# Token-major products in 512 output columns instead of 256, and dilated queries and keys written in residue order

## The chip, the cores and the metric

The kernel runs on one core of one Trainium2 chip. The metric is device time in microseconds (us) for one execution. TensorE is called PE here (its weight loads PEld), VectorE DVE, ScalarE ACT, GpSimd POOL, and SyncE, which issues most DMAs, SP.

## The reference

A network of three layers works on 512 tokens of width 1024, all in float32. Layer A mixes gated linear attention and dilated attention, then has an MLP and a gated embedding. Layer B mixes an mLSTM and stick-breaking attention; layer C has trailing-window pools and a projection. What the change touches:

```
hatt = (rmsnorm(x) @ w_in)[..., attention columns]     # [512, 3 groups, q/k/v, 4 heads, 128]
for g, (win, dil) in enumerate(((128, 1), (512, 4), (2048, 16))):
    # query t attends to t, t-dil, ..., within the window; keys gathered by stride dil
    out_g, lse_g = dilated_attention(q_g, k_g, v_g, bias_g, dil, win // dil)
o_att = sum over g of softmax(lse)_g * out_g
v_gla  = rmsnorm(x) @ w_in[:, 1024 columns]            # gated linear attention
va, vb = rmsnorm(x1) @ w_in_ab[:, 1024 columns each]   # mLSTM, stick-breaking
out    = x2 + rmsnorm((mixed * silu(z)) @ w_out_c)     # [512, 2048] @ [2048, 1024]
```

## The kernel before

**Products.** Activations lie feature-major: a tile holds 128 features on partitions and 512 tokens. Every float32 operand of a projection is split into a high and a low part of a narrower kind (`split`, ACT writes the high part, DVE the low one), and a product is three matmuls, high*high, high*low and low*high (`mm3`, L450 on; `mm`, L156, issues each, so nearly all PE work has line L157). Each matmul has its own weight load.

**Weights** stream from memory in chunks of 128 x 1024 (512 KB), 314 of them, in the order of use. `load_chunk` (L204) issues the DMA on SP, `split_chunk` splits it. Three raw and four split chunks fit (`RAW_BUFS`, `HL_BUFS`), so a chunk is split once the chunk four before it is used up.

**Units.** Each chunk is one unit of PE work. `fm` makes a feature-major tile [128 columns, 512 tokens]: 24 matmuls with 128 weight columns as the stationary operand and 512 tokens moving, into one bank of PSUM. `tok` makes a token-major output: here the *activations* are the stationary operand, 128 tokens at a time (j = 0 to 3), and 256 weight columns move; a chunk holds four k-tiles of 256 columns and needs 48 matmuls. Its four outputs of 256 columns share two banks. With `z` set (attention groups 1 and 2), token tile j holds the tokens j, j+4, j+8, ...: the weight load then reads every fourth element of the activation tile. `by_token` (only the last output columns of layer C) goes through the last two chunks once per token tile, so that a tile's output can leave while PE works on the next.

**Token-major outputs.** The values of the attention, for two pairs of heads and three groups (`v_units(pair, g)`; six of 256 columns, 4 of them with `z`), the values of the gated linear attention (4), VA and VB of layer B (4 each, one of each in each round `a0` to `a3`), and the final output (4, with 16 k-tiles in place of 8).

**PSUM.** Eight banks: four in the pool `mm` for the units, taken in turn, and four in the pool `q` for side work. A unit's result leaves its bank by its evacuation, on ACT or DVE.

**Side work** (attention, gla, mlstm, stick, one generator per head) advances by stages: `pump` runs once per unit, a slot, and lets a stage go once its slots (`LAG`) have passed and banks are free. A planner of the framework then puts the instructions of each engine in order by its own estimate of when they are ready, so a later matmul can stand ahead of an earlier one.

**Attention.** `qk_unit` writes a head's queries and keys for each group in the order of tokens, by one DVE instruction from PSUM. For groups 1 and 2, `attention` multiplies residue class by residue class, `zs(q[g])[:, z]` with `zs(k[g])[:, z]`, plain float32: both operands are read with a stride of four elements. Two records in the trace are one such product.

**Layer B, round a.** Four units of queries and keys for the mLSTM, each evacuated by DVE (a product with `rb_`, then three multiply-adds of a convolution), then VA (2 units), VB (2 units), and two pairs of units for the stick-breaking heads.

Of the kernel before, what the change touches and what calls it, by code (L numbers as in the profile page):

```python
# [17 lines left out]
P = 128  # L18
# [24 lines left out]
# key tile j meets the queries from WIDE[j][1] on, WIDE[j][0] of them, in bank and column PLACE[j]  # L43
# [6 lines left out]
# slots of 2 KB: for the units and for two kinds of side work  # L50
# [10 lines left out]
# slots that side work lets pass before each of its stages  # L61
# [4 lines left out]
N_ONEHOT = sum(BIASW)  # L66


class Net:
# [15 lines left out]
    # ---- storage  # L85
# [25 lines left out]
    # ---- engine shorthands  # L111
    # while set, an engine takes its instructions in the order in which they are written
# [8 lines left out]
    # each x (with its bias) becomes ln(1 + exp(-|x|)), in one table set  # L121
# [65 lines left out]
    # zero where the query is not after (or not at or after) the key  # L187
# [12 lines left out]
    # ---- the weight stream  # L200
# [19 lines left out]
    # a load that takes its turn in the weight stream  # L220
# [3 lines left out]
    # ---- program building  # L224
# [3 lines left out]
    # joint: so many units of the group advance together over their k-tiles, then the others in turn;  # L228
    # halves: all of them for the first half of the tokens, then for the second
# [12 lines left out]
    # Side work is a generator per head. It yields (slots to let pass, banks of the side  # L242
    # pool that it is about to take, condition) before each of its stages on the tensor engine.
# [80 lines left out]
    # a feature-major output tile [128 columns, 512 tokens] over 8 k-tiles  # L324
# [23 lines left out]
    # at most 64 columns: their weights come twice, and the low parts take the place of the second  # L348
    # ones, so that one pass of the array serves both parts
# [27 lines left out]
    # several feature-major tiles with few k-tiles in one chunk  # L377
# [26 lines left out]
    # a token-major output of 256 columns: chunks of four k-tiles; z: tokens in residue order;  # L404
    # by_token: so many last chunks are gone through once per token tile
    def tok(self, wname, lead, col, xs, z, evac, nk=8, by_token=0):
        st = {}
        parts = nk // 4
# [6 lines left out]
        def out(j):  # L415
            if by_token:
                return st["ps"][j][:, 0:256]
            return st["ps"][j // 2][:, (j % 2) * 256:(j % 2) * 256 + 256]

        fs = {}  # L420

        def mk(part):
            def emit(h, l):
                if part == 0:
                    st["ps"] = [self.MM(), self.MM()]
                    if by_token:
                        st["ps"] += [self.Q(), self.Q()]
                for k in range(4):
                    xh, xl = xs[part * 4 + k]
                    w = slice(k * 256, (k + 1) * 256)  # L430
                    for j in range(4):
                        s = part == 0 and k == 0 and (by_token > 0 or j % 2 == 0)
                        e = part == parts - 1 and k == 3
                        fs[part, k, j] = lambda o=out(j), a=(sel(xh, j), sel(xl, j)), b=(h[:, w], l[:, w]), s=s, e=e: (
                            self.mm3(o, a, b, s, e))
                if part < parts - by_token:
                    return [[fs[part, k, j] for j in range(4)] for k in range(4)]
                if part < parts - 1:
                    return [[]]
                return [[fs[p, k, j] for p in range(parts - by_token, parts) for k in range(4)]  # L440
# [3 lines left out]
        def ev():  # L444
            for j in range(4):
                evac(j, out(j))
# [5 lines left out]
        for u in us[:parts - by_token]:  # L452
            self.group(u)
# [1192 lines left out]
```

## Time and profile before

| What | Value |
|---|---|
| median of three timed runs | 1991.83 us (1990.28 to 1995.2) |
| profiled execution, first to last instruction (span) | 1988.3 us |
| PE busy | 1968.5 us, 99% |
| PEld busy | 1700.9 us, 86% |
| DVE busy, ACT busy | 1086.8 us (55%), 870.6 us (44%) |

The page gives no time of the profiled execution beyond its span; the median of the timed runs lies 3.5 us above it. An engine's busy time is the union of its instructions. Where instructions of one kind follow each other without a gap, the time of one is found as (busy time less the duration of one) / (count less one): each instruction lasts longer than the distance to the next, because they overlap.

### The profile page before, as it was taken

What the parts mean: (1) busy time and instruction counts of PE and PEld (TensorE: products, weight loads), DVE (VectorE), ACT (ScalarE), POOL (GpSimd) and SP (SyncE); (2) the same over time, 40 slices, a digit from 0 to 9 for tenths busy, and PEclk for the clock granted to TensorE, in tenths of its full rate; (3) what the DMA queues carried; (4) which work ended last, traced back from release to release, by engine and by line L of the source; (5) the groups of instructions that cost most, each with busy time, mean ns of one, the idle gap of its engine ahead of it and who ended that gap; (6) DMA issues with size and microseconds to landing.
All of it is one profiled execution on the core that took longest, in us unless ns stands there. A gap on an engine that the chain in (4) does not pass through costs nothing.

```text
span 1988.3 us, 25237 instructions
## 1 busy us (share of the span) xinstructions
PE 1968.5 (99%) x10142; PEld 1700.9 (86%) x10142; DVE 1086.8 (55%) x1647; ACT 870.6 (44%) x1325; POOL 94.3 (5%) x125
## 2 busy tenths in 40 slices
PE   8999999999999999999999999999999999999998
PEld 7989889888888888888888988898898888888898
DVE  5042253467744643344447767676857726666733
ACT  4132234456423432243235757576656534433322
POOL 0000000000000100000103001010000011000000
PEclk9999999999999999999999999999999999999999
DMA  5231232222234233333323322222222331333331
GB/s 180 82 92 54 80 91 75 85 75 75 85 95 138 96 96 95 101 104 95 96 96 117 107 75 86 86 84 74 81 90 75 107 115 64 99 102 96 95 107 64
DMA packets 68105, 184.47 MB, mean 93 GB/s; under 512 B 17058, under 2 KB 20815, under 8 KB 67988
## 3 DMA queue, kind: packets, MB, share of 16 engines
q1 hardware_dynamic: 67412, 181.82, 29.1%
q8 instruction: 79, 1.29, 0.3%
q10 hardware_dynamic: 576, 1.05, 0.1%
q14 instruction: 38, 0.31, 0.1%
HBM read 178.55 MB, written 6.12 MB: 93 GB/s over the span
## 4 chain that ended last, share of the span: by engine, by line
PE 95%; DVE 2%; ACT 1%; DMA 1%; issue 0%; SPq 0%; POOL 0%; DVEq 0%; ACTq 0%; POOLq 0%
PE t L157 95%; DVE t L136 2%; ACT t L119 1%; DVE t L148 0%; PE t L984 0%; DMA t<-t 0%; DMA t<-wstream 0%; PE t L1552 0%; POOL t L508 0%; PE t L1056 0%; SPq L537 0%; SPq L534 0%; DVEq L1642 0%; ACT t L1531 0%; SPq L523 0%
## 5 line engine op out<-in xcount | busy, mean ns | idle before, releaser
L157 PE MATMUL t<-t,t 128*128 128x512 f32 (+1 forms) x9780 | 1928.3, 359 | 13.9 <-ACT t L119 9.2
L157 PEld LDWEIGHTS t<-t,t 128*128 128x128 f32 x9780 | 1654.5, 196 | 275.4 <-ACT t L119 11.3
L136 DVE TENSOR_TENSOR t<-t,t 128x512 f32<-128x512 f32 (+10 forms) x990 | 769.9, 805 | 743.4 <-ACT t L119 415.6
L119 ACT ACTIVATE t<-t 128x512 f32<-128x512 f32 (+7 forms) x887 | 636.5, 756 | 942.6 <-PE t L157 565.7
L148 DVE SCALAR_TENSOR_TENSOR t<-t,t 128x512 f32<-128x512 f32 (+6 forms) x112 | 73.7, 675 | 97.1 <-PE t L157 60.5
L148 DVE SCALAR_TENSOR_TENSOR t<-t,ct,t 128x512 f32<-128x512 f32 (+5 forms) x128 | 102.3, 813 | 12.6 <-ACT t L119 9.7
L119 ACT ACTIVATE t<-t,t 128x256 f32<-128x256 f32 (+3 forms) x129 | 56.2, 464 | 105.6 <-PE t L157 72.2
L119 ACT ACT_TABLE_LOAD x61 | 78.3, 1283 | 8.9 <-DVE t L148 2.9
L508 POOL TENSOR_TENSOR t<-t,t 128x512 f32<-128x512 f32 x33 | 52.5, 1598 | 564.7 <-ACT t L119 564.4
L119 ACT ACTIVATE t<-t,ct 128x512 f32<-128x512 f32 (+5 forms) x89 | 54.8, 625 | 18.4 <-DVE t L136 12.9
L191 POOL TENSOR_SCALAR_AFFINE_SELECT t<-t 128x128 f32<-128x128 f32 (+1 forms) x80 | 36.6, 473 | 435.8 <-DVE t L148 221.2
L148 DVE SCALAR_TENSOR_TENSOR t<-t,t,t 128x256 fp32r<-128x256 f32 (+3 forms) x57 | 30.4, 549 | 14.7 <-ACT t L119 14.4
L136 DVE TENSOR_TENSOR t<-t 128x511 f32<-128x511 f32 (+5 forms) x64 | 37.4, 589 | 1.2
L482 DVE RECIPROCAL t<-t 128x512 f32<-128x512 f32 (+3 forms) x15 | 28.1, 1870 | 11.1 <-ACT t L119 10.9
L157 PE MATMUL t<-t,ct 128*128 128x256 f32 (+4 forms) x142 | 28.5, 336 | 0.0
L157 PEld LDWEIGHTS t<-t,ct 128*128 128x128 f32 (+1 forms) x142 | 21.6, 186 | 3.1 <-issue 0.7
L1531 ACT ACTIVATE t<-t 128x256 f32<-128x256 f32 x16 | 6.0, 379 | 29.7 <-PE t L157 26.4
L127 ACT ACT_TABLE_LOAD x13 | 16.7, 1283 | 0.2
L901 DVE CUSTOM_DVE_ANT_0 t<-t,t 128x128 f32<-128x128 f32 (+1 forms) x48 | 12.8, 318 | 5.8 <-PE t L157 5.7
L130 ACT ACTIVATE t<-t 128x512 f32<-128x512 f32 (+2 forms) x29 | 15.7, 594 | 0.1
L157 PEld LDWEIGHTS t<-ct,t 128*128 128x128 f32 x112 | 15.1, 200 | 0.5
L157 PE MATMUL t<-ct,t 128*128 128x1 f32 (+1 forms) x112 | 15.0, 264 | 0.0
(55 smaller groups left out, 136.1 us busy)
## 6 DMA issues: line engine op xcount, KB each, us to landing
t<-wstream SPq DMA_DIRECT2D x314, 512.0 KB
t<-xT SPq DMA_DIRECT2D x16, 256.0 KB
xdram<-t SPq DMA_DIRECT2D x8, 256.0 KB
t<-udram SPq DMA_DIRECT2D x8, 256.0 KB
t<-xdram SPq DMA_DIRECT2D x8, 256.0 KB
out<-t ACTq DMA_DIRECT2D x4, 256.0 KB
out<-t SPq DMA_DIRECT2D x4, 256.0 KB
skew<-bdram SPq DMA_DIRECT2D x2, 510.0 KB
```

The costliest lines, as they stand in the source:

```text
L119: self.pinned(self.nc.scalar.activation(out, in_, func, **kw))
L127: last = self.nc.scalar.preload_act_table_set(EXPLN)
L130: last = self.nc.scalar.activation(o, o, AF.Exp, scale=-1.0)
L136: self.pinned(self.nc.vector.tensor_tensor(out, a, b, op=op))
L148: self.pinned(self.nc.vector.scalar_tensor_tensor(out, a, s, b, op0=op0, op1=op1))
L157: self.nc.tensor.matmul(out, lhsT, rhs, start=start, stop=stop, skip_group_check=True)
L191: self.nc.gpsimd.affine_select(t[:, 0:n], t[:, 0:n], pattern=[[1, n]], compare_op=op, fill=0.0, base=base, channel_multiplier=-1)
L482: self.nc.vector.reciprocal(out, out)
L508: self.nc.gpsimd.tensor_tensor(st[key], st[key], sq, op=ALU.add)
L901: nc.vector.tensor_tensor_reduce(dst[:, lo:lo + n], ps[:, lo:lo + n], bias, scale=1.0, scalar=-3e38, op0=ALU.add, op1=ALU.max, accum_out=m ...
L1531: last = nc.scalar.activation(sq[:, 0:256], ps, AF.Square, accum_out=ss[j][:, c:c + 1])
```

## The change

Three edits. `tok` takes 512 columns (`pieces` may join two blocks of 256 from two matrices): a chunk holds two k-tiles, a matmul moves 512 columns, each token tile has a bank of its own out of `mm`, and every token-major output now goes through its last two chunks once per token tile (`TAIL`), as one group of two units. Attention values are made for all four heads at once, all before the first head's attention; VB is made together with VA. And `qk_unit` writes groups 1 and 2 in residue order, so that `attention` reads contiguous tiles.

```diff
-    def tok(self, wname, lead, col, xs, z, evac, nk=8, by_token=0):
+    def tok(self, pieces, xs, z, evac, nk=8):
...
                 if part == 0:
-                    st["ps"] = [self.MM(), self.MM()]
...
+                    st["ps"] = [self.MM() for _ in range(4)]
+                for k in range(2):
+                    xh, xl = xs[part * 2 + k]
+                    w = slice(k * T, (k + 1) * T)
                     for j in range(4):
...
+                if part < parts - TAIL:
+                    return [[fs[part, k, j] for j in range(4)] for k in range(2)]
                 if part < parts - 1:
                     return [[]]
+                return [[fs[p, k, j] for p in range(parts - TAIL, parts) for k in range(2)]
+                        + [lambda j=j: evac(j, st["ps"][j])] for j in range(4)]
...
+        for u in us[:parts - TAIL]:
             self.group(u)
+        self.group(*us[parts - TAIL:])
...
         def qk_unit(h, g, which, pre=None):
...
+                o, ps, r = (t, ps, self.r1) if g == 0 else (
+                    t.rearrange("p (z i) -> p z i", z=4), zs(ps), zs(self.r1))
                 if which == "q":
-                    self.stt(t, ps, P ** -0.5, self.r1)
+                    self.stt(o, ps, P ** -0.5, r)
                 else:
-                    self.mul(t, ps, self.r1)
+                    self.mul(o, ps, r)
...
         for g in range(3):
-            v_units(0, g)
+            v_units(g)
         self.go(self.attention(0, AT, VT))
         qk_head1(1)
         self.go(self.attention(1, AT, VT))
-        for g in range(3):
-            v_units(1, g)
...
-                self.mm(ps[:, z * P:(z + 1) * P], zs(q[g])[:, z], zs(k[g])[:, z], z == 0, True)
+                self.mm(ps[:, z * P:(z + 1) * P], q[g][:, z * P:(z + 1) * P], k[g][:, z * P:(z + 1) * P],
+                        z == 0, True)
...
         def rnd_a(i):
             qk_ml(i)
-            v_units(VA, B_VA, i)
+            v_units(i)
             self.go(self.mlstm(i, ML, VA))
-            v_units(VB, B_VB, i)
             qk_sb(2 * i)
...
-        for c in range(4):
+        for c in range(2):
             def evac(j, ps, c=c):
...
-            self.tok("w_out_c_2", 0, c * 256, mixed, False, evac, nk=16, by_token=TAIL if c == 3 else 0)
+            self.tok([("w_out_c_2", 0, c * T, T)], mixed, False, evac, nk=16)
```

## Rows read from the trace of the kernel before

**Rows 1.** The page's first two parts: busy time by engine, and the clock granted to PE in 40 slices.

```profile
PE 1968.5 (99%) x10142; PEld 1700.9 (86%) x10142; DVE 1086.8 (55%) x1647; ACT 870.6 (44%) x1325; POOL 94.3 (5%) x125
...
PEclk9999999999999999999999999999999999999999
```

**Rows 2.** The chain that ended last, by engine (page, part 4), and the list of waits for PE's matmuls alone: total us, times, longest.

```profile
PE 95%; DVE 2%; ACT 1%; DMA 1%; issue 0%; SPq 0%; POOL 0%; DVEq 0%; ACTq 0%; POOLq 0%
```

```profile
PE t L157 <- ACT t L119: 9.2, 6, 5.1
PE t L157 <- DVE t L148: 3.1, 4, 1.6
PE t L157 <- DVE t L136: 1.5, 1, 1.5
PE t L984 <- DVE t L152: 0.4, 1, 0.4
```

**Rows 3.** Groups of instructions by form in the stretch 60 to 100 us, attention values of groups 1 and 2 (`z` set): matmuls, weight loads. Columns: count | busy us, mean ns of one | idle before.

```profile
L157 PE MATMUL t<-t,t 128*128 128x256 f32 x173 | 40.5, 396 | 0.0
L157 PEld LDWEIGHTS t<-t,t 128*128 128x128 f32 x173 | 40.5, 329 | 0.0
```

**Rows 4.** The same view, matmuls of token-major outputs in order of tokens: 311 to 327 us (gated linear attention), 1246 to 1255 us (layer B, with its weight loads), 1910 to 1960 us (the output).

```profile
L157 PE MATMUL t<-t,t 128*128 128x256 f32 x136 | 16.5, 283 | 0.0
L157 PE MATMUL t<-t,t 128*128 128x256 f32 x78 | 9.5, 283 | 0.0
L157 PEld LDWEIGHTS t<-t,t 128*128 128x128 f32 x77 | 9.3, 192 | 0.0
L157 PE MATMUL t<-t,t 128*128 128x256 f32 x429 | 50.5, 280 | 0.0
```

**Rows 5.** The same view, matmuls of 512 columns: 600 to 1000 us (MLP of layer A, two lines), 1570 to 1640 us (end of layer B), 1800 to 1850 us (layer C).

```profile
L157 PE MATMUL t<-t,t 128*128 128x512 f32 x1742 | 400.3, 392 | 0.0
L157 PE MATMUL t<-t,ct 128*128 128x512 f32 x2 | 0.6, 389 | 0.0
L157 PE MATMUL t<-t,t 128*128 128x512 f32 x311 | 70.7, 389 | 0.0
L157 PE MATMUL t<-t,t 128*128 128x512 f32 x222 | 50.5, 389 | 0.0
```

**Rows 6.** The same view, column sums for the norms, one moving column each, so that the weight load alone sets the distance: 26.2 to 28 us (tokens mostly in residue order), 1092 to 1093.4 us (in order of tokens).

```profile
L157 PE MATMUL t<-ct,t 128*128 128x1 f32 x10 | 2.2, 347 | 0.0
L157 PEld LDWEIGHTS t<-ct,t 128*128 128x128 f32 x9 | 2.1, 312 | 0.0
L157 PE MATMUL t<-ct,t 128*128 128x1 f32 x15 | 1.7, 245 | 0.0
L157 PEld LDWEIGHTS t<-ct,t 128*128 128x128 f32 x14 | 1.6, 192 | 0.0
```

**Rows 7.** The same view, plain float32 products of 128 columns: 110.7 to 114.0 us (head 0's logits of groups 1 and 2, both operands strided), 415.5 to 418 us (gated linear attention, contiguous).

```profile
L157 PE MATMUL t<-t,t 128*128 128x128 f32 x15 | 3.7, 412 | 0.0
L157 PE MATMUL t<-t,t 128*128 128x128 f32 x25 | 3.0, 275 | 0.0
```

**Rows 8.** Round a0 of layer B. Matmuls by form, 1100.6 to 1111.7 us (the last two units before VA) and 1112.1 to 1117.4 us (VA's first unit); then DVE in order of time (start us, us, ...): the queue in between, and the instruction that empties the bank of the last unit before VA.

```profile
L157 PE MATMUL t<-t,t 128*128 128x512 f32 x51 | 11.8, 391 | 0.0
L157 PE MATMUL t<-t,t 128*128 128x256 f32 x46 | 5.7, 283 | 0.0
```

```profile
1111.63 0.75 DVE L148 SCALAR_TENSOR_TENSOR t<-t,ct,t 128x511 f32<-128x511 f32 x1 [2.53 <-ACT t L119]
...
1117.88 1.21 DVE L1274 TENSOR_TENSOR_SCAN t<-t,t 4x512 f32<-4x512 f32 x1
...
1122.05 0.67 DVE L136 TENSOR_TENSOR t<-t,t 128x512 f32<-128x512 f32 x1
```

**Rows 9.** DVE in order of time, the same instruction in rounds a1, a2 and a3, where VA's first unit begins at about 1230.5, 1311.4 and 1437.5 us, and the one ahead of the first attention values, which begin at 45.5 us.

```profile
1232.00 0.68 DVE L136 TENSOR_TENSOR t<-t,t 128x512 f32<-128x512 f32 x1
1311.76 0.63 DVE L136 TENSOR_TENSOR t<-t,t 128x512 f32<-128x512 f32 x1
1439.61 0.68 DVE L136 TENSOR_TENSOR t<-t,t 128x512 f32<-128x512 f32 x1
45.68 0.69 DVE L136 TENSOR_TENSOR t<-t,t 128x512 f32<-128x512 f32 x1 [3.35 <-PE t L157]
```

**Rows 10.** SP in order of time from 47.8 us (start us, us from the first issue to the end of the last), and a table of stretches: busy us of PE, PEld, DVE, ACT, POOL (count), PEclk, DMA share, GB/s.

```profile
47.80 0.36 SPq L204 DMA_DIRECT2D t<-wstream  x1
51.17 0.93 SPq L868 DMA_DIRECT2D bdram<-t  x2
52.88 10.76 SPq L873 DMA_DIRECT2D skew<-bdram  x3
63.74 9.11 SPq L204 DMA_DIRECT2D t<-wstream  x3
72.90 2.65 SPq L882 DMA_DIRECT2D t<-skew  x2
```

```profile
74.00:82.00 8.00, 8.00 (x36) 8.00 (x36) 0.00 (x0) 1.47 (x4) 0.00 (x0) 1.00 0.52 156
82.00:110.00 28.00, 28.00 (x124) 26.96 (x124) 0.76 (x2) 4.74 (x8) 0.00 (x0) 1.00 0.01 3
```

**Rows 11.** DVE in order of time: an addition that writes and reads SBUF with a stride of four elements, and one without stride behind it.

```profile
344.60 1.11 DVE L136 TENSOR_TENSOR t<-t,t 128x512 f32<-128x512 f32 x1 [1.10 <-PE t L157]
346.41 0.69 DVE L136 TENSOR_TENSOR t<-t,t 128x512 fp32r<-128x512 f32 x1 [0.70 <-ACT t L119]
```

**Rows 12.** The end, all engines in order of time: the last token tile's square, product and rows; then ACT's group of 512-column instructions over the whole span.

```profile
1982.82 0.38 ACT L1531 ACTIVATE t<-t 128x256 f32<-128x256 f32 x1 [2.01 <-PE t L157]
1983.10 0.19 ACT L1531 ACTIVATION_READ_ACCUMULATOR t<-t 128x1 f32 x1
1983.32 0.42 DVE L136 TENSOR_TENSOR t<-t,t 128x256 f32<-128x256 f32 x1 [0.87 <-ACT t L1531]
1983.66 0.15 DVE L1518 RECIPROCAL t<-t 128x1 f32<-128x1 f32 x1
```

```profile
L119 ACT ACTIVATE t<-t 128x512 f32<-128x512 f32 x293 | 172.7, 609 | 36.6 <-PE t L157 16.0 <-DVE t L136 14.5 <-DVE t L148 2.8
```

More of the change, by code (lines that the diff above doesn't have):

```diff
@@ L66, with zs @@
 N_ONEHOT = sum(BIASW)
+def zs(t):
+    return t.rearrange("p (i z) -> p z i", z=4)
 class Net:
@@ L431, in emit @@
                     for j in range(4):
-                        s = part == 0 and k == 0 and (by_token > 0 or j % 2 == 0)
-                        e = part == parts - 1 and k == 3
-                        fs[part, k, j] = lambda o=out(j), a=(sel(xh, j), sel(xl, j)), b=(h[:, w], l[:, w]), s=s, e=e: (
+                        s = part == 0 and k == 0
+                        e = part == parts - 1 and k == 1
+                        fs[part, k, j] = lambda o=st["ps"][j], a=(sel(xh, j), sel(xl, j)), b=(h[:, w], l[:, w]), s=s, e=e: (
@@ L435, in emit @@
                             self.mm3(o, a, b, s, e))
-                if part < parts - by_token:
-                    return [[fs[part, k, j] for j in range(4)] for k in range(4)]
+                if part < parts - TAIL:
+                    return [[fs[part, k, j] for j in range(4)] for k in range(2)]
                 if part < parts - 1:
                     return [[]]
-                return [[fs[p, k, j] for p in range(parts - by_token, parts) for k in range(4)]
-                        + [lambda j=j: evac(j, out(j))] for j in range(4)]
@@ L442, in mk @@
-            return emit
-        def ev():
-            for j in range(4):
-                evac(j, out(j))
+                return [[fs[p, k, j] for p in range(parts - TAIL, parts) for k in range(2)]
+                        + [lambda j=j: evac(j, st["ps"][j])] for j in range(4)]
+            return emit
         us = []
         for part in range(parts):
-            b = [(wname, lead, (part * 4 + k) * P, col, 256) for k in range(4)]
-            us.append(self.unit(b, mk(part), ev if part == parts - 1 and not by_token else None))
@@ L452, in tok @@
-        for u in us[:parts - by_token]:
+            b = [(name, lead, (part * 2 + k) * P, col, n) for k in range(2) for name, lead, col, n in pieces]
+            us.append(self.unit(b, mk(part)))
+        for u in us[:parts - TAIL]:
             self.group(u)
-        if by_token:
-            self.group(*us[parts - by_token:])
+        self.group(*us[parts - TAIL:])
     def mm3(self, out, a, b, start, stop):
@@ L594, in layer_a @@
         AT = [{"q": [None] * 3, "k": [None] * 3} for _ in range(4)]
-        VT = [[None] * 3 for _ in range(2)]
+        VT = [None] * 3
         def qk_unit(h, g, which, pre=None):
@@ L1516, in out_rows @@
             r = self.M(1)
-            self.act(r, ss[j][:, 3:4], AF.Sqrt, scale=1.0 / D, bias=ss[j][:, 4:5])
+            self.act(r, ss[j][:, 1:2], AF.Sqrt, scale=1.0 / D, bias=ss[j][:, 0:1])
             nc.vector.reciprocal(r, r)
@@ L1523, in out_rows @@
                     self.io["out"][j * P:(j + 1) * P, i * T:(i + 1) * T], y)
[L1525 removed]
+        for c in range(2):
             def evac(j, ps, c=c):
[L1527 to L1529 removed]
+                Yt[j][c] = self.S()
                 sq = self.S()
[L1531 to L1537 removed]
+                last = nc.scalar.activation(sq, ps, AF.Square, accum_out=ss[j][:, c:c + 1])
+                self.mul(Yt[j][c], ps, self.pgb[c])
+                if c == 0:
+                    self.ts(ss[j][:, 0:1], ss[j][:, 0:1], 1.0 / D, ALU.mult, EPS, ALU.add)
+                    if j == 3:
                         with self.tc.issue_after(last.ins):
                             nc.scalar.preload_act_table_set("sqrt_and_others")
[L1540 removed]
+                else:
                     out_rows(j)
[L1542 removed]
+            self.tok([("w_out_c_2", 0, c * T, T)], mixed, False, evac, nk=16)
     def transpose_x(self):
```

64 lines of the change are left out of this document (16 added, 48 removed).

## The prediction

> **What bounds the kernel now.** I read the busy times first: PE is busy 99% of the span, DVE 55%, ACT 44%, with PE's granted clock at its upper level in all forty slices [rows 1]. Then the chain of waits: 95% of it is PE, and all of PE's own waits come to 14.2 us [rows 2]. So PE's queue is the kernel's length, and the other engines matter only where they make PE wait. A busy PE says nothing of its pace, so I read that next, by form and by stretch. In a run without gaps the distance from one matmul to the next is (busy less one duration) / (count less one).
>
> - Values in residue order, 256 columns: (40.5 - 0.396) / 172 = 0.233 us [rows 3].
> - Token order, 256 columns: (16.5 - 0.283) / 135 = 0.120 in layer A, (9.5 - 0.283) / 77 = 0.120 in layer B, (50.5 - 0.280) / 428 = 0.117 at the output [rows 4].
> - 512 columns: (400.3 - 0.392) / 1743 = 0.229 in layer A, (70.7 - 0.389) / 310 = 0.227 in layer B, (50.5 - 0.389) / 221 = 0.227 in layer C [rows 5].
>
> The same 256 columns take twice as long when the activations are read with a stride of four elements. What sets that pace is the weight load: it lasts 329 ns in place of 192 [rows 3, 4], and where only one column moves, the distance is (1.7 - 0.245) / 14 = 0.104 us in token order but (2.2 - 0.347) / 9 = 0.206 in a stretch most of whose loads are strided [rows 6]. So 0.233 is about what a strided load takes by itself, with 256 columns or with one beside it.
>
> **Part 1: half as many matmuls for the residue values.** The four `tok` calls with `z` have 4 x 96 = 384 matmuls, 384 x 0.233 = 89.5 us. Afterwards there are 2 x 96 = 192 of 512 columns. The loads are still strided; the trace shows no strided load beside 512 moving columns. From below: the larger of 0.233 and 0.229, since with 256 columns the moving half lay wholly under the load [rows 3]. From above: load and stream one after the other, 0.233 + 0.229 = 0.462. I take 0.233, the nearest row being the same load with the same kind of stream: 192 x 0.233 = 44.7, a gain of 44.8 us. At the other end the gain is 0.8 us.
>
> The Trainium skill, "TensorE: Matmul & The Clock Gate", Part 3, "The mechanism", says that a weight load overlaps matmuls in flight only when the two use different row groups; full-array work like this would then pay the sum, 0.462 us. Against it, 256 columns at 0.120 us and a contiguous load of 0.104 by itself [rows 4, 6] do not add to 0.224, so I hold the rule to be too strict here; what it would make of the time is a rival below.
>
> **Part 2: half as many matmuls in token order.** Two of 256 become one of 512. Layer A: 96 pairs (group 0) and 192 (gated linear attention), 288 x (2 x 0.1201 - 0.2294) = 3.1 us. Layer B: 384 x (2 x 0.1197 - 0.2268) = 4.8. Output: 384 x (2 x 0.1173 - 0.2267) = 3.0. Together 10.9 us [rows 4, 5].
>
> **Part 3: contiguous logits.** A head has 8 products for groups 1 and 2, 16 records in the trace, at (3.7 - 0.412) / 14 = 0.235 us; contiguous products of the same size follow at (3.0 - 0.275) / 24 = 0.114 [rows 7]. 4 x 16 x 0.121 = 7.8 us. These lie on the path, as PE has no gap around them. The price moves to DVE: 16 evacuations (four heads, two groups, q and k) now read PSUM and `r1` with a stride. No row has a strided PSUM read; the strided addition took 1.11 us against 0.69 [rows 11]. I take 0.42 us more each, 6.7 us of DVE in layer A, where DVE has room; between nothing and twice that it hides behind units of 24 x 0.229 = 5.5 us.
>
> The Trainium skill, "SBUF — State Buffer", "Door 1: The DMA port swizzle", says that one can stride for free up to four fp32 elements. Read so, part 3 would gain nothing; the 0.235 against 0.114 above says that a stride of four is not free.
>
> Gross gain: 44.8 + 10.9 + 7.8 = 63.5 us.
>
> **Part 4: four banks in place of two.** A `tok` now takes all four `mm` banks, so its token tile j = 3 needs the bank of the unit just before it. That matmul is due after 9 others, 9 x 0.229 = 2.1 us, and behind it stand, in order, all of PE's work. What is late is the evacuation of that unit:
> - Round a0: the last unit before VA ends at about 1111.8 us (only 256-column matmuls from 1112.1 on), but DVE, full of the gates' scans and the convolutions of earlier units, empties its bank at 1122.05 + 0.67 = 1122.7. Due at 1113.9: 8.8 us late [rows 8].
> - a1: emptied at 1232.7, due 1232.6; a2: 1312.4, due 1313.5; a3: 1440.3, due 1439.6, 0.7 late [rows 9].
> - First attention values: emptied at 46.4, due 47.6, no wait [rows 9].
>
> Before, two other banks were free and nothing waited. The planner can put VA's other token tiles and its next chunk first, if it foresees the delay: 0 to 8.8 us for a0. I take the middle, 4.4, and 0.8 for a1 and a3. After a `tok` the next unit needs the bank of j = 0, emptied three tiles earlier: nothing.
>
> **Part 5: grouped tails.** The last two chunks of all 11 `tok` are one group: `pump` runs twice in front of it, so side work due within those slots stands one unit (5.5 us) nearer to its inputs. The one stage of side work that PE is seen to wait for, the transposes of L984, waited 0.4 us [rows 2]. Bounds: nothing, or about 5.5 us for each of a few; I take 1 us. Both split chunks of the group come free only at its end, while two more stand ready, 11 us of work: enough for two splits.
>
> **Part 6: the weight stream after 45 us.** 11 chunks after the first two were issued up to 47.8 us; then SP is held by the bias tables' copies until 63.7, and three chunks go out by 72.9 [rows 10]. Counting from 0, these are 13, 14 and 15. So far the slow residue units gave cover; now PE wants chunk 13 near 45.5 + 15 x 2.3 = 80 us (each token tile's tail takes 12 x 0.229 = 2.7, so this is within a few us). The DMA engines are half busy to 82 us and then empty, so all has landed by then [rows 10]. Taken as no wait; at worst 82 + 2.3 for its split, 4.3 us late.
>
> **Part 7: the end.** The last tile's square and product cover 512 columns. From the square's start to the reciprocal it was 0.84 us; the square grows from 0.38 to about 0.61, the product from 0.42 to about 0.69: 0.5 us more [rows 9, 12].
>
> Sum: -63.5 + 4.4 + 0.8 + 1 + 0.5 = -56.8. Span 1988.3 - 56.8 = 1931.5; the timed median lies 3.5 above the span, so 1935 us.
>
> **The rivals.**
> 1. *PE waits for banks and chunks in several places*: a0 in full (8.8 us), two more rounds of layer B at half that, the stream's 4.3 us. 1935 + 4.4 + 8.8 + 4.3 = 1952. For it: DVE is densest just where layer B's `tok` begin [rows 8]; against it, three of the four rounds show lags of 2 to 3 us [rows 9]. Chance 0.12.
> 2. *A strided load is not hidden beside 512 columns*: part 1 gains 0.8 in place of 44.8, 1935 + 44 = 1979. For it: no row has the two together. Against it: 256 columns are hidden under the same load [rows 3]. Chance 0.06. It is what the rule of the Trainium skill weighed in part 1 would make of the time.
> 3. *Slower*: every one of the 11 `tok` waits for its fourth bank as long as a0's, 11 x 8.8 = 97, less 63.5 and plus 1.5: 2027 with the 1991.8 of now. It decides from 63.5 / 11 = 5.8 us each; only a0 is seen above that. Chance 0.03.
> 4. *More than forecast*: no wait at all, and fewer semaphores or side work falling better gives a few us beyond 1991.8 - 63.5 = 1928, to 1922. Chance 0.05.
>
> **How the numbers follow.** The forecast has 0.74; its own range is 1926 to 1944 (part 4 at 0 or in full, part 5 at 0 to 5, the logits' and pairs' paces give 2 either way). To take in the rivals next to it I widen to 1924 to 1953: it holds nearly all of the forecast's share and most of rival 1's, about 0.82. A measurement of this kernel tells 0.3%, 6 us, from no change. Faster by more: 0.95; within: 0.02; slower: 0.03.
>
> **What would show each step.** Matmuls of 512 columns with weight loads of 329 ns should follow at 0.233 us between 67 and 112 us (0.46 would be rival 2, any step between measures part 1). Token-order `tok` should run at 0.227 to 0.229. The 16 logit records of a head should take about 1.8 us, with weight loads of 192 ns, and the 16 evacuations between 0.7 and 1.6 us. A gap on PE with DVE L136 as releaser, near the start of VA in round a0, would be part 4; one with ACT or DVE behind a wstream DMA before 85 us, part 6; waits at L984 or at layer B's side work, part 5. The prediction is wrong if the time lies above 1953, or if it is met with part 1 well off 44.8 us and something else making up for it.

## The result: 1936.93 us, and the profile after

The changed kernel takes 1936.93 us (median of 4 runs, 1935.65 to 1938.06), the kernel before beside it 1991.38 (1990.28 to 1995.2): ratio 0.9722, 95% interval 0.971 to 0.9734, or 54.5 us less. 1935 was predicted, 1924 to 1953. The profiled spans, 1988.3 and 1934.9, differ by 53.4 us; the sum had 56.8.

The page after: busy times (as [rows 1]), granted clock, and the chain that ended last (as [rows 2]).

```profile
PE 1911.9 (99%) x8894; PEld 1597.9 (83%) x8894; DVE 1090.2 (56%) x1623; ACT 873.2 (45%) x1274; POOL 94.7 (5%) x125
...
PEclk9999999999999999999999999999999999999999
...
PE 94%; DVE 3%; ACT 1%; DMA 1%; issue 0%; SPq 0%; POOL 0%; DVEq 0%; ACTq 0%; POOLq 0%
```

PE lost 56.6 us of busy time and 1248 records; what it waits for, in the list of waits after, grew a little:

```profile
PE t L162 <- ACT t L124: 9.8, 6, 5.1
PE t L162 <- DVE t L153: 3.2, 5, 1.6
PE t L162 <- DVE t L141: 2.5, 1, 2.5
PE t L1264 <- DVE t L141: 1.4, 1, 1.4
```

(L162 is `mm`, L157 before; L141, L153 and L124 are L136, L148 and L119.) So 16.9 us in place of 14.2. New are the 1.4 at L1264, the transposes of the gates in round a0 of layer B, and 2.5 in place of 1.5 late in layer B (near 1499 us).

Where the time went, by the starts of the same PE work in the two traces (differences are taken before rounding):

| stretch | before, us | after, us | difference | predicted |
|---|---|---|---|---|
| to the first product in question | 45.5 | 45.5 | 0 | 0 |
| layer A up to its MLP | 460.8 | 404.8 | -56.0 | -44.8 - 3.1 - 7.8 = -55.7 |
| MLP and embedding | 587.3 | 588.2 | +0.9 | 0 |
| layer B | 596.0 | 597.5 | +1.5 | -4.8 + 4.4 + 0.8 = +0.4 |
| layer C up to the output | 202.9 | 202.7 | -0.1 | 0 |
| output | 90.2 | 90.2 | -0.1 | -3.0 |
| end | 5.6 | 6.0 | +0.4 | +0.5 |

The prediction's one further microsecond (part 5, grouped tails) was given to no stretch and stands in no row.

Groups by form after, in 92 to 117 us, inside the residue values (as [rows 3]): matmuls, weight loads.

```profile
L162 PE MATMUL t<-t,t 128*128 128x512 f32 x107 | 25.5, 400 | 0.0
L162 PEld LDWEIGHTS t<-t,t 128*128 128x128 f32 x107 | 25.4, 316 | 0.0
```

(25.5 - 0.400) / 106 = 0.237 us for one, where 0.233 was taken and 0.462 was the upper bound. A strided load of 316 ns stands beside each product, and the product of 512 columns hides nearly all of it.

### The profile page after: what moved, and what is told of

It reads as the page before. It is cut to its first block, busy times and chain, and to the rows that moved or that the text cites. A ratio compares the mean times of both kernels' runs of the same rounds, so it can differ in the third digit from the quotient of the medians.

```text
span 1934.9 us, 22678 instructions
## 1 busy us (share of the span) xinstructions
PE 1911.9 (99%) x8894; PEld 1597.9 (83%) x8894; DVE 1090.2 (56%) x1623; ACT 873.2 (45%) x1274; POOL 94.7 (5%) x125
## 4 chain that ended last, share of the span: by engine, by line
PE 94%; DVE 3%; ACT 1%; DMA 1%; issue 0%; SPq 0%; POOL 0%; DVEq 0%; ACTq 0%; POOLq 0%
PE t L162 93%; DVE t L141 2%; ACT t L124 1%; DMA t<-t 1%; DVE t L153 1%; PE t L965 0%; DMA t<-wstream 0%; PE t L1528 0%; ACT L124 0%; POOL t L499 0%; PE t L1037 0%; SPq L528 0%; ACT L135 0%; DVE t L1252 0%; SPq L525 0%
## 5 line engine op out<-in xcount | busy, mean ns | idle before, releaser
L162 PE MATMUL t<-t,t 128*128 128x512 f32 (+3 forms) x8532 | 1871.5, 381 | 15.7 <-ACT t L124 9.8
L162 PEld LDWEIGHTS t<-t,t 128*128 128x128 f32 x8532 | 1550.0, 192 | 323.2 <-ACT t L124 13.4
L141 DVE TENSOR_TENSOR t<-t,t 128x1024 fp32r<-128x1024 f32 (+9 forms) x982 | 773.1, 815 | 730.4 <-ACT t L124 404.1
L124 ACT ACTIVATE t<-t 128x1024 fp32r<-128x1024 f32 (+6 forms) x883 | 633.5, 758 | 924.3 <-PE t L162 557.6
L153 DVE SCALAR_TENSOR_TENSOR t<-t,ct,t 128x512 f32<-128x512 f32 (+5 forms) x128 | 102.5, 815 | 14.4 <-ACT t L124 11.2
L153 DVE SCALAR_TENSOR_TENSOR t<-t,t 128x512 f32<-128x512 f32 (+6 forms) x112 | 76.5, 702 | 54.2 <-PE t L162 45.8
L124 ACT ACTIVATE t<-t,t 128x128 f32<-128x128 f32 (+4 forms) x93 | 50.3, 545 | 62.8 <-PE t L162 36.7
L124 ACT ACTIVATE t<-t,ct 128x512 f32<-128x512 f32 (+5 forms) x89 | 54.8, 624 | 19.4 <-DVE t L141 12.8
L196 POOL TENSOR_SCALAR_AFFINE_SELECT t<-t 128x128 f32<-128x128 f32 x80 | 37.4, 482 | 418.3 <-ACT t L124 222.5
L141 DVE TENSOR_TENSOR t<-t 128x511 f32<-128x511 f32 (+5 forms) x64 | 37.3, 587 | 1.2
L153 DVE SCALAR_TENSOR_TENSOR t<-t,t,t 128x512 fp32r<-128x512 f32 (+3 forms) x41 | 27.7, 683 | 13.1 <-ACT t L124 12.8
L162 PE MATMUL t<-t,ct 128*128 128x256 f32 (+4 forms) x142 | 28.6, 337 | 0.0
L162 PEld LDWEIGHTS t<-t,ct 128*128 128x128 f32 (+1 forms) x142 | 21.6, 186 | 3.6 <-issue 1.0
L130 ACT ACTIVATE t<-t 128x512 f32<-128x512 f32 (+2 forms) x25 | 12.4, 561 | 10.3 <-PE t L162 7.7
L162 PEld LDWEIGHTS t<-ct,t 128*128 128x128 f32 x112 | 16.5, 217 | 0.6
L162 PE MATMUL t<-ct,t 128*128 128x1 f32 (+1 forms) x112 | 16.2, 276 | 0.0
L1509 ACT ACTIVATE t<-t 128x512 f32<-128x512 f32 x8 | 4.8, 599 | 24.7 <-PE t L162 24.7
L135 ACT ACTIVATE t<-t 128x512 f32<-128x512 f32 (+2 forms) x29 | 15.8, 594 | 0.2
```

The lines of the kernel that those rows point to most:

```text
L124: self.pinned(self.nc.scalar.activation(out, in_, func, **kw))
L130: last = self.nc.scalar.activation(o, x, AF.Abs, bias=bias)
L135: last = self.nc.scalar.activation(o, o, AF.Exp, scale=-1.0)
L141: self.pinned(self.nc.vector.tensor_tensor(out, a, b, op=op))
L153: self.pinned(self.nc.vector.scalar_tensor_tensor(out, a, s, b, op0=op0, op1=op1))
L162: self.nc.tensor.matmul(out, lhsT, rhs, start=start, stop=stop, skip_group_check=True)
```

## The experiments

In what follows a run is held against the kernel before and the changed kernel. The kernel before, timed beside every set of runs, had medians of 1991.38 to 1991.85 us; the changed kernel's 1936.93 is from the first set.

**The strided load: before and after.** In both kernels the values of groups 1 and 2 are computed in token order: the runs leave out the residue order of these rows, so their outputs are not the network's, but counts and shapes stay.

```diff
-            self.tok("w_in", 0, col, xs, g > 0, evac)                                 # before
+            self.tok("w_in", 0, col, xs, False, evac)
-            self.tok([("w_in", 0, A_ATT + g * 1536 + 1024, T)], xs, g > 0, evac)      # after
+            self.tok([("w_in", 0, A_ATT + g * 1536 + 1024, T)], xs, False, evac)
```

> The kernel before with the values of groups 1 and 2 computed in token order: the part of the computation that changes is the order of the rows of these values; all counts and shapes stay, and so do the 256 columns, the two banks and the logits. My theory (before, each of the 384 products of these values was held up by its strided load): they fall from 0.233 to the 0.120 of the other 256-column products, 384 x 0.113 = 43.4 us faster, about 1948.5, 41 to 46. Rival (the gain of the change in this stage came from half as many instructions and from the evacuations, and the load is only part of it): 10 to 30 us faster.

Measured: 1947.13 us, 44.3 less than before, ratio 0.9778 (0.9762 to 0.9794); the span fell by 43.9. Groups of this run in 60 to 78 us:

```profile
L157 PE MATMUL t<-t,t 128*128 128x256 f32 x152 | 18.4, 283 | 0.0
L157 PEld LDWEIGHTS t<-t,t 128*128 128x128 f32 x151 | 18.2, 192 | 0.0
```

(18.4 - 0.283) / 151 = 0.120 us, with the load back at 192 ns. 384 x (0.233 - 0.120) = 43.4 us was what the stride cost before, all of it. Taking the stride away from the 256-column kernel gives almost what the 512 columns give; the 512 columns don't shorten the load, they cover it.

> The changed kernel with the values of groups 1 and 2 computed in token order: the part of the computation that changes is the order of the rows of these values, the count and the shape of every instruction stay. The 192 products of these values then load contiguous weights. My theory (the strided load of about 0.31 us lies wholly beside 512-column products): the pace falls from 0.236 to the 0.227 of other 512-column products, 192 x 0.009 = 1.7 us faster, 1 to 2.5, about 1935.2. Rival (part of the strided load still shows, as the 40 ns over 0.227 at some of the products): 5 us or more faster.

Measured: 1933.29 us, 3.6 less than the changed kernel, ratio 0.9705 (0.9692 to 0.9718). Groups in 92 to 117 us:

```profile
L162 PE MATMUL t<-t,t 128*128 128x512 f32 x112 | 25.5, 389 | 0.0
L162 PEld LDWEIGHTS t<-t,t 128*128 128x128 f32 x110 | 20.7, 188 | 4.3
```

(25.5 - 0.389) / 111 = 0.226, so the strided load costs about 0.011 us beside 512 columns, 192 x 0.011 = 2 us in all. The rest isn't in these products. Set side by side, the two traces differ by 2.2 us over these products and by 1.2, 1.0, 1.6 and 3.1 us, of both signs, in four places where the work is the same: the loads of the first 48 us, and the gaps near 1030, 1500 and 1630 us, where the granted clock differs (below). Rival 2 of the prediction, that the load isn't hidden, is out.

**The logits: undone in the changed kernel, and alone in the one before.**

```diff
-                o, ps, r = (t, ps, self.r1) if g == 0 else (
-                    t.rearrange("p (z i) -> p z i", z=4), zs(ps), zs(self.r1))
...
-                    self.mul(o, ps, r)
+                    self.mul(t, ps, self.r1)
...
-                self.mm(ps[:, z * P:(z + 1) * P], q[g][:, z * P:(z + 1) * P], k[g][:, z * P:(z + 1) * P],
+                self.mm(ps[:, z * P:(z + 1) * P], zs(q[g])[:, z], zs(k[g])[:, z], z == 0, True)
```

> The changed kernel with the queries and keys of the dilated groups back in token order, so that the 64 records of logits (16 a head) read their weights with a stride of four again; everything else as changed. My theory: 64 records at 0.235 in place of 0.106 us, none hidden, so 8.3 us slower on TensorE, less 0.3 to 1 us if the shorter evacuations release something: 7 to 8.5 us slower, about 1944.5. Rival (the records stand where TensorE would have waited anyway for the softmax behind them): 0 to 3 us slower, and new waits named at the logits' evacuations in place of the saved time. Second rival (the strided read of PSUM by VectorE, which the change added, costs the path more than the records saved): 1 us or more faster.

Measured: 1944.89 us, 8.0 more than the changed kernel, ratio 0.9762 (0.9748 to 0.9775). The logits of head 1, as [rows 7], first in this run (163.0 to 166.5 us), then in the changed kernel (160.0 to 161.7):

```profile
L162 PE MATMUL t<-t,t 128*128 128x128 f32 x15 | 3.7, 412 | 0.0
```

```profile
L162 PE MATMUL t<-t,t 128*128 128x128 f32 x15 | 1.8, 275 | 0.0
```

(3.7 - 0.412) / 14 = 0.235 against (1.8 - 0.275) / 14 = 0.109 us: 64 x 0.126 = 8.1 us, as measured. The price was paid by DVE, off the path: a strided evacuation takes 1.08 us (the changed kernel at 135.30 us, in order of time) in place of 0.69 [rows 9], 0.39 more against the 0.42 taken.

```profile
135.30 1.08 DVE L153 SCALAR_TENSOR_TENSOR t<-t,t 128x512 f32<-128x512 f32 x1 [3.30 <-PE t L162]
```

> The kernel before with the third part of the change alone: queries and keys of the dilated groups written in residue order, 256-column products as before. Nothing of the computation changes. My theory (64 records of logits at 0.106 in place of 0.235 us, all on the path, and the longer evacuations beside TensorE's work): 7 to 8.5 us faster, about 1984, as much as undoing it cost in the changed kernel. Rival (before, the strided records lay beside waits that the other part of the change removed): 0 to 4 us faster.

Measured: 1986.3 us, 5.1 less than before, ratio 0.9969 (0.9959 to 0.9979), between the two theories. The span fell by only 3.9. Set beside the trace of before, PE gains 1.9 us behind each head's logits, 7.7 in all, and 1.5 more between heads 0 and 1; it loses 2.1 in the loads of the first 47 us, and 3.2 in two places behind a gap, at 1070 to 1090 and 1670 to 1690 us. Tables of these stretches (PE busy, count, PEclk, DMA share, GB/s), this run and the one before:

```profile
1070.00:1090.00 20.00, 16.45 (x99) 0.83 0.27 88
1670.00:1690.00 20.00, 17.36 (x93) 0.83 0.32 105
```

```profile
1075.00:1095.00 20.00, 16.21 (x112) 0.91 0.23 80
1675.00:1695.00 20.00, 17.18 (x101) 0.91 0.32 106
```

A mean of 0.83 over 20 us is 6.8 us at the lower level (1.2 of 2.4 GHz), 0.91 is 3.6. So the logits' gain is there, and in this profile the two stretches behind a gap took 3.2 back. The timed runs say the same: the mean granted clock over the whole kernel is 0.9956 in the eleven of this run and 0.9967 in the fifteen of the kernel before beside it. A thousandth of the clock is some 2 us here (an estimate: at half speed, as much time is lost as the mean lies below 1), so at the same clock the logits alone would be worth about 7 us, as my theory had it. Why one execution has the longer stretch is open.

**The grouped tails and the wait at the gates.**

```diff
-            us.append(self.unit(b, mk(part)))
-        for u in us[:parts - TAIL]:
+            us.append(self.unit(b, mk(part), ev if part == parts - 1 and not tail else None))
+        for u in us[:parts - tail]:
             self.group(u)
-        self.group(*us[parts - TAIL:])
+        if tail:
+            self.group(*us[parts - tail:])
...
-            self.tok([("w_out_c_2", 0, c * T, T)], mixed, False, evac, nk=16)
+            self.tok([("w_out_c_2", 0, c * T, T)], mixed, False, evac, nk=16, tail=c * TAIL)
```

> The changed kernel with every chunk of a token-major unit as a group of its own and the four evacuations behind the last one, except for the very last unit of the kernel, which keeps its order by token tile. Nothing of the computation changes. My theory (the grouped tails cost next to nothing on the path, about 1 us in all, and move the steps of side work by a chunk, so that the wait of 1.39 us at the transposes of the gates goes away): between 3 us faster and 1 us slower, about 1935.5. Rival (without the tails each unit that follows another waits for its banks: three places in layer A, three in layer C and the GLA values, 1 to 2.5 us at each): 4 to 10 us slower, with waits on ScalarE's copies named at the first products of the units.

Measured: 1936.09 us, ratio 0.9719 (0.9706 to 0.9732): the same as the changed kernel. Both halves of the theory can be read off the waits: no new wait on ScalarE, and the one at the gates still there.

```profile
PE t L162 <- ACT t L124: 9.1, 5, 5.1
PE t L162 <- DVE t L153: 3.3, 5, 1.6
PE t L162 <- DVE t L141: 2.5, 1, 2.5
PE t L1269 <- DVE t L141: 1.4, 1, 1.4
```

So the tails cost nothing that can be measured, and they are not what made the wait at the gates. That part of my theory fell.

```diff
-LAG = {..., 'ml_gates': (5,), ...}
+LAG = {..., 'ml_gates': (6,), ...}
```

> The changed kernel with the transposes of the mLSTM gates let one slot later (5.5 us of TensorE work more between the chain that makes the gates and the transposes that read them). Nothing of the computation changes. My theory (the wait of 1.39 us at 1062.4 us exists because the grouped tail brings the step a slot forward): the wait goes, 1.4 us faster, up to 2.3 if the longer stretch at the lower clock that begins near it goes too, about 1935.2. Rival (the wait is only put off, since mLSTM's first steps need the transposed gates): no change, and a wait on VectorE of about 1 us at the weights of mLSTM.

Measured: 1938.43 us, ratio 0.9731 (0.9718 to 0.9745): no gain. PE in order of time:

```profile
1055.68 10.36 PE L162 MATMUL t<-t,t 128*128 128x512 f32 x45
1065.97 0.41 PE L1264 MATMUL t<-ct,t 4*128 4x4 f32 x4
1066.31 0.50 PE L162 MATMUL t<-t,t 128*128 128x512 f32 x1
1068.09 6.20 PE L162 MATMUL t<-t,t 128*128 128x512 f32 x26 [1.28 <-DVE t L141]
```

The transposes no longer wait, but PE stops for 1.28 us one product later. DVE, in order of time in the same run, shows behind what:

```profile
1062.53 0.67 DVE L141 TENSOR_TENSOR t<-t,t 4x512 f32<-4x512 f32 x1
1063.13 0.73 DVE L153 SCALAR_TENSOR_TENSOR t<-t,ct,t 128x511 f32<-128x511 f32 x1
1063.80 1.20 DVE L1254 TENSOR_TENSOR_SCAN t<-t,t 4x512 f32<-4x512 f32 x1
1064.93 0.71 DVE L153 SCALAR_TENSOR_TENSOR t<-t,ct,t 128x510 f32<-128x510 f32 x1
1065.57 0.67 DVE L141 TENSOR_TENSOR t<-t,t 4x512 f32<-4x512 f32 x1
1066.17 0.73 DVE L153 SCALAR_TENSOR_TENSOR t<-t,ct,t 128x509 f32<-128x509 f32 x1
1066.83 2.94 DVE L141 TENSOR_TENSOR t<-t,t 128x1024 fp32r<-128x1024 f32 x3
```

DVE has no gap here. A 128x1024 subtraction makes the low part of a weight chunk, which the second product of a chunk is the first to need; at its usual 1.2 us the first of the group ends at 1068.0, just before PE goes on, and it stands behind the gates' scans and the convolutions. Both waits have one cause: in round a0, DVE's queue sets the end, and PE arrives about 1.3 us early at either place. The rival was right that the wait is only put off, but it is put off to the weights' split, not to the mLSTM.

**The pace of 512 columns.** The output was to gain 3.0 us and gained 0.1. The groups after, 720 to 780 us (second half of the MLP's products) and 1860 to 1920 (output):

```profile
L162 PE MATMUL t<-t,t 128*128 128x512 f32 x259 | 60.6, 395 | 0.0
...
L162 PE MATMUL t<-t,t 128*128 128x512 f32 x258 | 60.6, 397 | 0.0
```

(60.6 - 0.397) / 257 = 0.234, not the 0.227 of layers B and C [rows 5]. Both stretches read activations from the side pools (two pools of tiles in SBUF, kinds `s` and `r`), which lie at the top of a partition; most other activations lie in the main pool. So the next runs move pools. A tile that is only named early claims its pool's place:

```diff
+        self.S(kind="s"), self.S(kind="r")                       # side pools low
         self.xt = [self.S() for _ in range(KT)]
```
```diff
+        for t in ("wh", "wl"):                                   # split weights low
+            self.sb.tile([P, 1024], F32R, name=self._nm(), tag=t, bufs=HL_BUFS)
         self.xt = [self.S() for _ in range(KT)]
```

> The changed kernel with the two side pools of tiles at the low addresses of a partition (18 to 82 KB), the main pool above them (82 to 170 KB) and the split weights at the top (182 to 214 KB, before at 118 to 150). Nothing of the computation changes. First theory (a 512-column product runs at 0.234 in place of 0.227 us when either of its operands lies above some 155 KB): the some 5800 products of a streamed weight with a tile of the main pool become slow, + 5800 x 0.0067 = 39 us, 30 to 42, about 1973. Second theory (only the activations' place counts): the second MLP products, the output and the other 1400 products that read the side pools fall to 0.227, 5 to 9 us faster, about 1930, less what the top of the main pool loses. Rival (place has nothing to do with it, but what these tiles hold or who wrote them): the same products stay at 0.234 and the time within 2 us.

> The changed kernel with the split weights at the low addresses of a partition (18 to 50 KB), the main pool at 50 to 138 KB and the side pools where they were (from 156 KB on). Nothing of the computation changes. First theory (0.234 when either operand lies above some 155 KB): the same products as before are slow, no change within 2 us. Third theory (0.234 only when both operands lie in the upper part, since before the weights lay at 118 to 150 KB and the side pools above): the slow products fall to 0.227, 6 to 9 us faster, about 1929.

Measured: side pools low 1924.27 us (1921.48 to 1925.72), ratio 0.9659 (0.9643 to 0.9674), 12.7 less than the changed kernel; weights low 1935.87, ratio 0.9719 (0.9704 to 0.9735), no change. With the side pools low the same two stretches (720 to 780, 1850 to 1910 us) are at (60.7 - 0.389) / 266 = 0.227:

```profile
L162 PE MATMUL t<-t,t 128*128 128x512 f32 x267 | 60.7, 389 | 0.0
...
L162 PE MATMUL t<-t,t 128*128 128x512 f32 x267 | 60.7, 389 | 0.0
```

The first theory falls (weights at 182 to 214 KB cost nothing), the third falls with the second run. The second was nearly met in time, but the main pool now reaches to 170 KB and its tiles above 155 KB are fast as well, so height can't be the cause. The programs' addresses suggested another: the side pools began 32 bytes past a multiple of 64 only where they were slow.

```diff
-        self.bif = self.C([36, 1])                        # side pools 32 bytes on
+        self.bif = self.C([36, 16])[:, 0:1]
-        self.vecs = self.C([P, NVEC])                     # all pools 32 (8) or 64 (16) bytes on
+        self.vecs = self.C([P, NVEC + 8])[:, 0:NVEC]
```

> The changed kernel with one constant of 32 bytes a partition made 64 bytes, so that the 32 tiles of the two side pools, and everything behind them, begin at a multiple of 64 bytes, as the main pool and the weights do, where they began 32 bytes past one. All pools keep their places and order; nothing of the computation changes. Fourth theory, from the run with the side pools low, in which these tiles happened to come to such multiples (a 512-column product with an operand that begins 32 bytes past a multiple of 64 runs at 0.234, with both at multiples at 0.227): the products of the side pools' tiles fall to 0.227 at their old addresses, 8 to 12 us faster, about 1926. Rival (it was the place, low against high, in some way that the two placement runs mixed): no change within 2 us.

> The changed kernel with the constant of vectors 32 bytes a partition longer, which moves everything behind it by 32 bytes: now the main pool and the split weights begin 32 bytes past a multiple of 64, and the side pools at multiples. Nothing of the computation changes. Fourth theory (an operand 32 bytes past a multiple of 64 costs some 0.0067 us per 512-column product): all products of a streamed weight are slow, those of the side pools' tiles with them; about 5800 more than in the changed kernel, 30 to 42 us slower, about 1972. Rival (the place): no change within 2 us.

> The changed kernel with both constants longer, so that the main pool, the weights and the side pools all begin at multiples of 128 bytes, where those at 0.227 began 64 past one. Nothing of the computation changes. Fourth theory as it stands (64 bytes is what counts): the same time as with the side pools at multiples of 64, about 1926, within 2 us. Rival (a finer multiple is better still): the pace of all 512-column products falls below 0.227, at 0.22 by some 7000 x 0.007 = 49 us more.

> The kernel before with the constant of 32 bytes made 64, so that its side pools begin at multiples of 64 bytes too. Nothing of the computation changes. Fourth theory: its second MLP products and the others of 512 columns on side tiles gain as in the changed kernel, 7 to 9 us; its output's 768 products of 256 columns, now at 0.117, keep their time or go to the 0.120 of the others (2.3 us more): 5 to 9 us faster, about 1984. If the output keeps 90 us here and falls to 87.2 in the changed kernel, the gain that the prediction gave the output was there and hidden by the tiles' place. Rival (the place): no change within 2 us.

Measured: sides 32 bytes on 1932.95 us, ratio 0.9698 (0.9681 to 0.9716); everything 32 bytes on 1936.98, ratio 0.9713 (0.9695 to 0.9731); all at multiples of 128, 1933.52, ratio 0.9702 (0.9684 to 0.972); the kernel before with its sides 32 bytes on 1995.65, ratio 1.0014 (1.0003 to 1.0024), so slightly slower than before, and not the 5 to 9 us faster that was expected. The fourth theory fell: the second of these has the main pool and the weights off 64 and nothing happens, and its output (1861 to 1921 us) is as slow as ever, though its side pools now begin at multiples of 64; so is that of the first (1856 to 1916 us), at 0.232:

```profile
L162 PE MATMUL t<-t,t 128*128 128x512 f32 x258 | 60.6, 396 | 0.0
```

```profile
L162 PE MATMUL t<-t,t 128*128 128x512 f32 x260 | 60.6, 395 | 0.0
```

The 4.0 and 3.4 us that the first and the third of these runs took less than the changed kernel are not in this pace. In the first one's profile the clock's means behind the two gaps are 0.91 and 1.00, where the changed kernel has 0.83 twice (tables below):

```profile
1020.00:1040.00 20.00, 16.23 (x111) 0.91 0.25 83
1620.00:1640.00 20.00, 17.36 (x107) 1.00 0.33 112
```

Set side by side, the two traces differ by 0.8 and 3.1 us at these places. The timed runs fit: their mean granted clock is 0.997 in all four of the first and 0.9965 over the third, 0.9955 in the changed kernel, by the estimate above some 3 and 2 us. The rest is not traced.

What is left is the place of the two operands against each other. I set the matmuls of six of these traces (the changed kernel and the five moved ones of its family) beside the addresses in their programs, took each pair of contiguous 512-column products that follow each other, and sorted by the distance, in bytes of a partition, from the tile that the second one loads to the tile that the first one streams:

```
distance modulo 256      pairs     mean distance in time, ns
0                        35432     227.1
96                        3324     233.4
128                       3028     233.0
160                       1234     234.0
```

All six fit: main pool and weights are multiples of 256 apart in every one; the side pools are 96 or 160 off in the changed kernel, with the weights low and with everything moved by 32, 128 off where the side pools moved by 32 against the rest, and 0 only with the side pools low. The seams, where the work goes over from one pool to another, show in the same six traces that this distance counts and not the place of the pool: 180 pairs whose distance is off, though the second product's own two tiles are a multiple of 256 apart, have a median of 232 ns; 130 pairs the other way round have 227.

The kernel before, sorted in the same way, has no such loss for 256 columns: pairs at distance 0 take 120 ns (0.120 in [rows 4]), 767 at 160 take 117.3, and 850 at 128, in its variant, 119.9. The 767 are the output, and the variant moved it from 160 to 128; its row in 1915 to 1965 us gives (50.4 - 0.283) / 418 = 0.120 for the 0.117 of [rows 4], 768 x 0.0026 = 2.0 us of the 3.8 that the variant lost.

```profile
L157 PE MATMUL t<-t,t 128*128 128x256 f32 x419 | 50.4, 283 | 0.0
```

That is the output's missing gain: before, its 256 columns happened to run at 2 x 117 = 234, after, its 512 at 234.

This rule was found by sorting the runs after they were made; no run was made to foretell it, and what in the chip it stands for is open.

## Why the prediction was right

- **Part 1** (44.8 us): right. The pace was 0.237 where 0.233 was taken, so 192 x 0.237 = 45.5 us are left of 89.5, a gain of 44.0. The choice between 0.233 and 0.462, by the nearest row, was the step on which most hung, and it held. The rule weighed there, that a load overlaps products in flight only when their row groups differ (the Trainium skill, "TensorE: Matmul & The Clock Gate", Part 3, "The mechanism"), this trace contradicts: 316 ns of load beside a product, and 0.237 for the two. The same section also lets a load into the background weight buffer go ahead of products in flight; with that the trace would agree.
- **Part 2** (10.9): right in layer A, where the whole stretch gave 56.0 against 55.7 (parts 1, 2 and 3 together). Wrong at the output: the step "384 x (2 x 0.1173 - 0.2267) = 3.0" took the pace of 512 columns from [rows 5], layer C, whose activations there lie in the main pool. The output's lie in the side pools, and there it is 0.234, which leaves nothing. The row was at hand: the MLP's 0.229 [rows 5] was a mean of 0.227 and 0.234, and I read it as one pace. With the side pools low, 384 x (0.234 - 0.227) = 2.7 us of the 3.0 come.
- **Part 3** (7.8): right, 8.1 by the rows and 8.0 by the run that undid it. DVE pays 0.39 us for each strided evacuation (0.42 taken) and hides it. The Trainium skill, "SBUF — State Buffer", "Door 1: The DMA port swizzle", has a stride of four fp32 as free; here it more than doubles the record, 0.235 against 0.109 us.
- **Part 4** (4.4 + 0.8): right in cause, DVE's queue in round a0; wrong in form. In the program's order VA's fourth token tile stands behind the other three and products of the next two chunks, so no product waited for a bank. Less of PE's work now stands ahead of the transposes of the gates, and PE waited 1.39 us there for the same queue:

```profile
1055.82 5.15 PE L162 MATMUL t<-t,t 128*128 128x512 f32 x22
1062.36 0.38 PE L1264 MATMUL t<-ct,t 4*128 4x4 f32 x4 [1.39 <-DVE t L141]
```

  Before, the last subtraction of the gates ended at 1116.61 + 0.67 = 1117.28 us and the transposes began at 1117.64: there was no slack to gain from. Late in layer B, too, 1.1 us went into a longer wait. The sum had layer B at 0.4 us slower and 1.5 was measured, but for other reasons than forecast: the products did gain, VA and VB of round a1 running at (21.5 - 0.389) / 93 = 0.227 us (1178.2 to 1199 us), but these two waits (2.5 us) and the clock (below) took the gain back, and no bank did. That the totals lie close is luck. Rival 1 weighed the lags of a1 to a3 as "2 to 3 us"; by [rows 9] that of a2 is 1.0.

```profile
L162 PE MATMUL t<-t,t 128*128 128x512 f32 x94 | 21.5, 389 | 0.0
```

- **Part 5** (1): nothing, by the run without tails. **Part 6** (none): no wait on the stream. The one new wait in this stretch, 0.7 us at 118.65 us, was for ScalarE's copy of the values, which stood behind an exponential that waited for a DMA; of the later profiles only one has part of it. **Part 7** (0.5): from the last square to the reciprocal 1.33 us, 0.49 more.
- **The clock**, in no part of the sum. The prediction read it as at its upper level throughout [rows 1], but a 9 there is 90% or more of a slice of some 50 us, which hides a stretch of a few us. The gaps near 1028 and 1627 us were there before, and so was a stretch at the lower level behind each, but in the changed kernel's profile it is about twice as long. Its table, to be held against that of the kernel before above, has the same 0.83:

```profile
1020.00:1040.00 20.00, 16.42 (x105) 0.83 0.22 81
1620.00:1640.00 20.00, 17.37 (x91) 0.83 0.33 106
```

  That is 6.8 - 3.6 = 3.2 us more at half speed in each, about 1.6 us of time by this reckoning. The MLP's row, in which no work was changed, grew by 0.9. At the second gap the same work, from 1675.54 to 1689.62 us before and 1619.47 to 1635.96 after, takes 2.4 us more. With the two waits that is 4.9 of the 6.3 us between layer B's 1.5 and the -4.8 of part 2; the other 1.4 is not traced. With the side pools low the stretches have 0.91 and 0.83:

```profile
1013.00:1033.00 20.00, 16.23 (x109) 0.91 0.25 87
1612.00:1632.00 20.00, 17.39 (x93) 0.83 0.32 106
```

The span missed the sum by 3.4 us: 2.9 at the output, 0.9 and 1.1 in the two rows that hold the clock's stretches, less 1.0 of part 5 and 0.5 of small gains. The median missed by only 1.9, since it lies 2.0 above the span where 3.5 was taken. So the median lies closer to the forecast than the mechanism does: the output's 2.9 us and the two longer stretches of the clock were foreseen by no part, and a smaller wait in a0 (1.4 us in place of 4.4) paid for some of them.

The version with the side pools low beats both kernels. Its median is 12.7 us below the changed kernel's, its profiled span 10.9. Of the span, 9.8 are the 1514 pairs of products that lay off a multiple of 256 in the changed kernel's trace, at 0.0063 to 0.0070 us each, and 0.9, with the traces side by side, falls where the first stretch at the lower clock is shorter.

## What to carry to other kernels

A slow weight load need not be shortened if the stream beside it is made long enough to cover it: compare the pace that the load sets by itself (here 0.233 us) with the pace of the stream (0.120 for 256 columns, 0.227 for 512), and widen the stream where the load is longer. A pace must be read from a stretch with the same pools on both sides of the product, since a mean over two pools hides two paces. Where an in-order queue without gaps feeds the path, as DVE's in round a0, time saved on the engine that waits for it turns into a wait, and moving the wait gains nothing.

## What was not expected of the hardware

- 512-column products ran at 0.227 us where the streamed and the loaded tile lay multiples of 256 bytes apart and at 0.233 to 0.234 where they did not, while 256-column ones ran at 0.120 and 0.117 to 0.120 in the two cases. One line that named two pools early made the kernel 12.7 us faster, some 10 of them by this pace.
- A load with a stride of four elements sets a pace of 0.233 us beside 256 columns, and costs about 0.011 us beside 512.
- After the same gaps, PE's clock stayed at the lower level for 3.6 us in some profiles of a kernel's family and 6.8 in others, and with the weights low it was not lower at 1622 to 1642 us at all (1.00), but at 1496 to 1516 (0.91).
